# Feed-forward layers as seven products of half blocks, with the residual and the inner operands in DRAM

## The chip, the cores and the metric

The kernel runs on one core of one Trainium2 chip. The metric is the time on the device of one execution, in microseconds (us); lower is better. Engines are named as in the profile: PE (matrix products), DVE (VectorE), ACT (ScalarE), POOL (GpSimd), SP (the queue that issues the DMAs).

## The reference, cut to what matters

A decoder of two layers over 1024 tokens of width 1024, all in float32. Each layer is `x += mixer(RMSNorm(x))`, then `x += SwiGLU(RMSNorm(x))`. The mixer of layer 0 has sixteen attention heads of two kinds, that of layer 1 eight differential heads; the change doesn't touch what they compute. The feed-forward part, which it does touch, has an inner width of 2816:

```python
def swiglu(h, w_gate, w_up, w_down):
    a = jnp.einsum('bsd,df->bsf', h, w_gate)
    u = jnp.einsum('bsd,df->bsf', h, w_up)
    return jnp.einsum('bsf,fd->bsd', jax.nn.silu(a) * u, w_down)
```

## The kernel before, in words

Activations lie transposed: 128 rows of the width by partition, the tokens along the row, in two halves of 512 (`th` 0 and 1). A float32 product is made of three passes in a one-pass number format: an operand x is split into a high part, which ACT writes as a cast, and a low part, which DVE or POOL writes as x minus the high part; `mm3` (L365) then issues high times high, high times low and low times high (L369, L370, L371) for each 128 rows of the contraction, a stationary block of 128 x 128 against a moving one of 128 x 512.

**Mixer.** `mixer` (L797) runs eight windows of attention, with projections and most of the output projection filled in between. `out_rest` (L963) follows it: the last two pieces' part of the output projection (6 matmuls for each of 16 pieces of x), the sum with x on DVE (L984), and `prep` (L306) of each piece: ACT multiplies by the norm's gain into the high part, DVE writes the low part (L315), ACT squares, and DVE or POOL adds up the squares (L321). `rms` (L324) makes 1 / rms of a half's tokens from that sum: a DVE add (L329), a split, two matmuls (L334, L335), Ln and Exp on ACT, and a Newton step on DVE (L343 to L345), into the row tile `rt`.

**Feed-forward.** The feed-forward (`ffn`, L1021) takes x times gain as it is and brings 1 / rms in behind the product, so its matmuls don't wait for `rms`. It goes through the inner width in groups of three or two chunks of 128. Of each chunk, `ffn_half` (L994) issues 24 matmuls for gate and 24 for up, for each half of the tokens; DVE, ACT, POOL (L1005) and DVE make silu(gate) times up, and ACT and DVE split it. Then `down` (L1011) multiplies the group's chunks into all eight pieces of the output and adds each result to x, which stays in SBUF (L1018, one operand in PSUM). Of layer 0's last group, `prep` and `rms` of the next norm follow piece by piece. In matmuls, gate and up are 22 chunks x 2 x 2 halves x 24 = 2112, down is 22 x 8 x 2 x 3 = 1056: 3168 in each layer.

**Weights.** `w_load` (L204) brings each weight tile by DMA into one of three raw tiles and splits it, the low part on DVE while a feed-forward runs and on POOL otherwise (`pool_split`); `w_ahead` keeps two to four tiles ahead, across the border between a feed-forward and the next mixer.

**Order and memory.** The text writes a program order. The framework then lays out each engine's instructions when it builds: among those that it expects to be ready it takes the one that stands first in the text. The order is fixed from then on; each engine and the SP queue go through theirs one by one, and wait where an operand isn't there. SBUF is 44 tiles of 4 KB by partition and some of 2 KB, made once, handed out and taken back by `Slots` (L48).

## Time and profile before

| | us |
|---|---|
| three runs | 2703.07, 2704.07, 2707.98 |
| median | 2704.07 |
| profiled execution, first to last instruction (span) | 2704.3 |
| PE busy in it | 2621.7 |
| DVE, ACT, POOL busy in it | 1550.8, 1111.2, 416.5 |

The page gives no other time of the profiled execution than its span; that is 0.2 us above the median of the runs. Busy time is a sum over the whole span; the feed-forward parts lie at about 660 to 1400 us and 1975 to 2701 us, the mixers ahead of each. A line number in a row is that of the code before; helpers (L84 and L92 are ACT's) gather many places under one line.

### The profile page before, as it was taken

Reading aid. Unit: us, or ns where it says so; the run is one execution under the profiler, and the core shown is the slowest. Engines: PE = TensorE matmul, PEld = TensorE weight load, DVE = VectorE, ACT = ScalarE, POOL = GpSimd, SP = SyncE. Lnnn points to the kernel's source line nnn. Section 1 sums busy time; section 2 is a strip of 40 time slices with the busy share of each in tenths; the row PEclk is TensorE's granted clock in tenths of the full one; section 3 lists DMA queues with packets and bytes.
Section 4 is the critical chain, followed back from the end, with each engine's and each line's share of the span. In section 5 each row is a group of like instructions: output and inputs, shape, how many; then the busy total and the mean of one; then the engine's idle time right before and its main releaser. Section 6 shows DMA issues by size and latency. Waiting matters only on the chain. (4 is left out here: it accounts for less than half of the span.)

```text
span 2704.3 us, 34626 instructions
## 1 busy us (share of the span) xinstructions
PE 2621.7 (97%) x12688; PEld 2159.9 (80%) x12688; DVE 1550.8 (57%) x3095; ACT 1111.2 (41%) x2276; POOL 416.5 (15%) x400
## 2 busy tenths in 40 slices
PE   8898899999999999999999999998999999999999
PEld 7776788777888888888878877876778888888887
DVE  6879868988333334333376687788663334333343
ACT  5656676755311211111156666676451211121111
POOL 4112111211100000000022232323110000000000
PEclk9999999999999999999999999999999999999999
DMA  5323042552111111111133232335311111111112
GB/s 182 85 61 80 28 129 79 146 172 81 50 52 46 49 47 53 49 40 55 43 121 86 77 97 74 80 100 156 125 39 45 50 47 55 48 43 54 46 50 79
DMA packets 118310, 202.61 MB, mean 75 GB/s; under 512 B 14163, under 2 KB 44660, under 8 KB 118140
## 3 DMA queue, kind: packets, MB, share of 16 engines
q1 hardware_dynamic: 118140, 200.41, 24.5%
q8 instruction: 99, 1.62, 0.2%
q14 instruction: 71, 0.58, 0.1%
HBM read 135.83 MB, written 22.58 MB: 59 GB/s over the span
## 5 line engine op out<-in xcount | busy, mean ns | idle before, releaser
L369 PE MATMUL bk<-sr,sr 128*128 128x512 f32 x2880 | 1129.7, 393 | 7.5 <-DVE hf L422 3.2
L370 PE MATMUL bk<-sr,sr 128*128 128x512 f32 x2880 | 1128.0, 392 | 4.2 <-DVE sr L922 4.2
L371 PE MATMUL bk<-sr,sr 128*128 128x512 f32 x2880 | 1126.7, 391 | 0.0
L369 PEld LDWEIGHTS bk<-sr,sr 128*128 128x128 f32 x2880 | 542.4, 188 | 121.7 <-DVE sf L1018 5.0
L370 PEld LDWEIGHTS bk<-sr,sr 128*128 128x128 f32 x2880 | 541.8, 188 | 114.1 <-DVE sr L922 5.8
L371 PEld LDWEIGHTS bk<-sr,sr 128*128 128x128 f32 x2880 | 542.1, 188 | 110.1 <-issue 0.4
L84 ACT CAST sr<-raw 128x512 fp32r<-128x512 f32 (+2 forms) x436 | 253.6, 587 | 648.2 <-PE bk L370 540.6
L218 DVE TENSOR_TENSOR sr<-raw,sr 128x512 fp32r<-128x512 f32 (+1 forms) x304 | 197.4, 650 | 237.0 <-ACT sr L84 221.6
L1005 POOL TENSOR_TENSOR hf<-hf,rt 128x512 f32<-128x512 f32 x88 | 114.4, 1300 | 1267.9 <-ACT hf L92 1267.9
L1018 DVE TENSOR_TENSOR sf<-bk,sf 128x512 f32<-128x512 f32 x256 | 176.2, 689 | 183.0 <-PE bk L371 182.7
L218 POOL TENSOR_TENSOR sr<-raw,sr 128x512 fp32r<-128x512 f32 (+2 forms) x132 | 177.0, 1349 | 354.6 <-ACT sr L84 171.5
L92 ACT ACTIVATE hf<-hf 128x512 f32<-128x512 f32 x200 | 125.5, 629 | 250.7 <-DVE hf L1003 247.9
L84 ACT CAST sr<-hf 128x512 fp32r<-128x512 f32 (+1 forms) x158 | 98.1, 621 | 294.7 <-DVE hf L1006 269.7
L1006 DVE TENSOR_TENSOR hf<-hf,bk 128x512 f32<-128x512 f32 x88 | 60.6, 688 | 252.9 <-PE bk L371 248.5
L560 PE MATMUL bk<-sr,sr 128*128 128x512 f32 (+2 forms) x768 | 200.0, 357 | 4.8 <-ACT sf L92 4.3
L682 PE MATMUL bk<-hr,sr 128*128 128x512 f32 (+2 forms) x560 | 166.0, 389 | 12.9 <-DVE hr L700 12.2
L84 ACT CAST hr<-bk 128x512 fp32r<-128x512 f32 (+2 forms) x240 | 122.4, 527 | 97.6 <-PE bk L668 86.7
L700 DVE TENSOR_TENSOR hr<-bk,hr 128x512 fp32r<-128x512 f32 (+2 forms) x240 | 142.3, 604 | 34.7 <-ACT hr L84 33.4
L1003 DVE TENSOR_TENSOR hf<-bk,rt 128x512 f32<-128x512 f32 x88 | 60.9, 691 | 172.2 <-PE bk L371 172.2
L560 PEld LDWEIGHTS bk<-sr,sr 128*128 128x128 f32 x768 | 127.9, 190 | 29.4 <-ACT sf L92 16.0
L462 PE MATMUL bk<-sr,sr 128*128 128x256 f32 (+1 forms) x512 | 147.2, 289 | 2.8 <-DVE sr L315 2.7
L668 PE MATMUL bk<-ident,sf 128*128 128x128 f32 x768 | 134.3, 276 | 15.3 <-DVE sf L580 11.4
(148 smaller groups left out, 2787.8 us busy)
## 6 DMA issues: line engine op xcount, KB each, us to landing
sr<-sr SPq DMA_DIRECT2D x96, 256.0 KB, 3.0
raw<-in_wg_dram SPq DMA_DIRECT2D x88, 256.0 KB, 2.8
raw<-in_wu_dram SPq DMA_DIRECT2D x88, 256.0 KB, 2.7
raw<-in_wd_dram SPq DMA_DIRECT2D x72, 256.0 KB, 2.7
raw<-in_w_dram SPq DMA_DIRECT2D x64, 256.0 KB, 2.9
sr<-sr SPq DMA_DIRECT2D x128, 128.0 KB, 2.3
sf<-od SPq DMA_DIRECT2D x14, 512.0 KB, 3.5
raw<-in_wd_dram SPq DMA_DIRECT2D x48, 128.0 KB, 2.2
```

The costliest lines, as they stand in the source:

```text
L84: self.last = self.e.copy(out, in_)
L92: self.last = self.e.activation(*args, **kw)
L218: (self.nc.gpsimd if self.pool_split else self.nc.vector).tensor_tensor(r32(l[:, m]), r, h[:, m], ALU.subtract)
L369: nc.tensor.matmul(ps, WH[k], hH[k], start=first and k == 0, stop=False)
L370: nc.tensor.matmul(ps, WH[k], hL[k], start=False, stop=False)
L371: nc.tensor.matmul(ps, WL[k], hH[k], start=False, stop=last and k == n - 1)
L462: nc.tensor.matmul(ps[:, 0:n], hl, vh[k], start=False, stop=k == KC - 1)
L560: nc.tensor.matmul(b[:, 0:hi - lo], r32(Q[i // 4][:, q]), r32(KK[:, lo:hi]), start=j == 0, stop=j == 1)
L668: nc.tensor.transpose(t[:, (i - 4 * g) * P:(i - 4 * g + 1) * P], w[:, kb * P:kb * P + P], self.ident[:])
L682: nc.tensor.matmul(ps[:, c1:], x, y, start=first and j == 0, stop=last and j == len(terms) - 1)
L700: self.nc.vector.tensor_tensor(r32(l[:, c0:]), src, h[:, c0:], ALU.subtract)
L1018: self.nc.vector.tensor_tensor(x, ps[:], x, ALU.add)
```

## The change: what it does

Each feed-forward product is written as a product of 2 x 2 half blocks, C = A B, and made of seven block products instead of eight (Strassen's method in the form with 15 sums). Of gate and up, A is a chunk of the two weights (rows: gate, up; columns: the even and the odd 128-row pieces of x) and B the normed x (rows: even and odd pieces; columns: the two halves of the tokens). Of down, A is a pair of chunks of its weight (rows: the two halves of the output's width; columns: the two chunks) and B the inner result of that pair.

- The work is a list of stages, each prepared (`prep_gate`, `prep_down`) and run (`gate`, `down`): 11 batches of two chunks x 7 products with 24 matmuls each, then three groups of 4, 4 and 3 pairs x 7 products with 12 matmuls for each pair. That is 1848 + 924 = 2772 matmuls in a layer. Preparing of gate and up goes three stages ahead, of down one.
- POOL makes the sums of weights (`left`: three at product 2, one at product 5, for each chunk or pair). ACT and DVE split every operand of every product (`split`).
- Products share PSUM banks in the order 0+1, 2+3, 4+5, 6 (down: 0+1, 2+3, 6, 4+5): the second product is added onto the first once ACT or DVE has taken the first out. `rE` has all eight banks.
- `out_rest` sends x to `y_dram`, no longer makes `prep`, and needs 1 / rms before it multiplies: x times gain times `rt` on DVE, in place, then split into B; the sums of B (two on DVE, two on POOL for each of four pieces) and their splits follow once both halves are there. 28 tiles of B stay for the layer.
- The inner result's seven operands of a pair (`hidden`: four DVE sums) go to `t_dram` and come back as they are needed (`take_right`).
- The output's x comes from `y_dram`, is added and goes back, for each group and piece (`add_x`: DVE where the product is in PSUM, POOL elsewhere); with the last group it goes to the output, or to `x_dram` and into the next `prep`.
- Feed-forward weights no longer pass through `w_load`; they are loaded whole (512 KB) and split by product. The weights of layer 1's mixer are no longer loaded during the feed-forward by the text.
- `Slots` hands out places, for which a new tile is made each time, and the pools are joined during a feed-forward. The raw tiles are four, of which the mixer holds one for what was `row3`.

```diff
+    def left(self, i, A, tmp):
+        p = self.nc.gpsimd
+        a11, a12, a21, a22 = A
+        if i == 2:
+            p.tensor_tensor(tmp, a21, a22, ALU.add)
+            p.tensor_tensor(a21, a11, a21, ALU.subtract)
+            p.tensor_tensor(a11, tmp, a11, ALU.subtract)
+        if i == 5:
+            p.tensor_tensor(a12, a12, a11, ALU.subtract)
+        return self.split((a11, a12, a11, a21, tmp, a12, a22)[i])
...
+    def split(self, x):
+        t = self.sr.get()
+        h, l = t[:, 0:TH], t[:, TH:2 * TH]
...
+        self.S.copy(r32(h), x)
+        self.nc.vector.tensor_tensor(r32(l), x, h, ALU.subtract)
+        return t
...
     def out_rest(self, l):
...
+        Slots.join(self.sr, self.sf)
+        Slots.join(self.hr, self.hf, self.raw)
+        self.take_raw(0)
...
                 nc.vector.tensor_tensor(x, ps[:], x, ALU.add)
-                if k < 6:
-                    self.prep(acc, x, G_FFN0 if l == 0 else G_FFN1, th, k)
-            for k in range(6, KC):
-                self.prep(acc, self.x_at(k, th), G_FFN0 if l == 0 else G_FFN1, th, k)
+                nc.sync.dma_start(self.y_dram[k][:, sl], x)
+                self.squares(acc, x, k, k < 2)
             self.rms(acc, th)
+            for k in range(KC):
+                x = self.x_at(k, th)
+                nc.vector.scalar_tensor_tensor(x, x, self.gains[:, g0 + k:g0 + k + 1], self.rt[:, sl],
+                                               ALU.mult, ALU.mult)
+                if th == 0:
+                    self.B[k % 2].append(self.split(x))
+            if th == 0:
+                self.prep_to(2)
...
+        for b11, b12, b21, b22 in xs:
+            nc.vector.tensor_tensor(b11, b12, b11, ALU.subtract)
+            nc.gpsimd.tensor_tensor(b12, b22, b12, ALU.subtract)
+            self.B[5].append(self.split(b22))
+            nc.vector.tensor_tensor(b22, b22, b11, ALU.subtract)
+            self.B[2].append(self.split(b22))
+            nc.gpsimd.tensor_tensor(b21, b21, b22, ALU.subtract)
+        for i, place in ((3, 1), (4, 0), (6, 2)):
+            for j in range(4):
+                self.B[i].append(self.split(xs[j][place]))
...
+    def gate(self, b, i, W):
...
+            if i == 0:
+                v["p"], v["s"] = self.hf.get(), self.hf.get()
+                self.S.copy(v["p"][:], ps)
+            elif i == 1:
+                self.S.activation(v["s"][:], ps, AF.Silu)
+            elif i == 2:
+                v["u"] = self.hf.get()
+                nc.vector.tensor_tensor(v["u"][:], ps, v["p"][:], ALU.add)
...
+            elif i == 5:
+                u = v["u"][:]
+                nc.vector.tensor_tensor(u, ps, u, ALU.add)
+                self.S.activation(u, u, AF.Silu)
+                nc.gpsimd.tensor_tensor(u, u, v["q"][:], ALU.mult)
+            else:
+                nc.vector.tensor_tensor(v["p"][:], ps, v["p"][:], ALU.add)
+                nc.gpsimd.tensor_tensor(v["s"][:], v["s"][:], v["p"][:], ALU.mult)
...
+    def down(self, g, s, ops):
...
+            if i == 0:
+                self.S.copy(p0, ps)
+            elif i == 1:
+                self.add_x(g, u, 0, ps, True)
+            elif i == 2:
+                nc.vector.tensor_tensor(u2, ps, p0, ALU.add)
+            elif i == 3:
+                nc.vector.tensor_tensor(p0, ps, p0, ALU.add)
+            else:
+                c = self.hf.get()
+                nc.vector.tensor_tensor(c[:], ps, u2 if i == 5 else p0, ALU.add)
+                self.add_x(g, 4 + u if i != 5 else u, 0 if i == 6 else 1, c[:], False)
+                self.hf.put(c)
...
+    def add_x(self, g, k, th, c, psum):
...
+        t = self.hf.get()
+        nc.sync.dma_start(t[:], self.y_dram[k][:, sl])
+        (nc.vector if psum else nc.gpsimd).tensor_tensor(t[:], c, t[:], ALU.add)
+        dst = self.y_dram[k] if not last else self.x_dram[k] if self.l == 0 else self.out[k * P:(k + 1) * P, :]
+        nc.sync.dma_start(dst[:, sl], t[:])
```

## Rows read from the trace of the kernel before

**Rows 1.** The page, part 1: engine, busy us (share), instructions.

```profile
PE 2621.7 (97%) x12688; PEld 2159.9 (80%) x12688; DVE 1550.8 (57%) x3095; ACT 1111.2 (41%) x2276; POOL 416.5 (15%) x400
```

**Rows 2.** Windows of 50 and 10 us: length, engines' busy us, granted clock, DMA share, GB/s.

```profile
670.00:680.00 10.00, 7.25 (x28) 5.59 (x27) 7.82 (x12) 5.61 (x7) 1.94 (x2) 0.89 0.20 66
...
700.00:750.00 50.00, 50.00 (x222) 41.39 (x221) 19.16 (x30) 11.42 (x19) 3.88 (x3) 1.00 0.17 58
...
2650.00:2700.00 50.00, 50.00 (x223) 41.38 (x222) 19.30 (x29) 6.25 (x10) 3.90 (x3) 1.00 0.23 83
```

**Rows 3.** Groups by line, PE alone, 690 to 1340 us.

```profile
L369 PE MATMUL bk<-sr,sr 128*128 128x512 f32 x956 | 371.9, 389 | 0.0
```

**Rows 4.** Groups by line and shape: busy us, mean ns, idle before and its releasers.

```profile
L84 ACT CAST sr<-raw 128x512 fp32r<-128x512 f32 x364 | 224.3, 622 | 603.7 <-PE bk L370 500.6 <-PE bk L371 43.0 <-DMA raw<-in_wu_dram 18.8
L218 DVE TENSOR_TENSOR sr<-raw,sr 128x512 fp32r<-128x512 f32 x256 | 177.0, 692 | 215.1 <-ACT sr L84 199.7 <-PE bk L370 13.0 <-PE bk L371 1.4
L1018 DVE TENSOR_TENSOR sf<-bk,sf 128x512 f32<-128x512 f32 x256 | 176.2, 689 | 183.0 <-PE bk L371 182.7
...
L1005 POOL TENSOR_TENSOR hf<-hf,rt 128x512 f32<-128x512 f32 x88 | 114.4, 1300 | 1267.9 <-ACT hf L92 1267.9
```

**Rows 5.** Timeline at layer 0's border, DVE and POOL: start us, us, engine, line.

```profile
641.25 0.74 DVE L315 SCALAR_TENSOR_TENSOR sr<-sf,gains,sr 128x512 fp32r<-128x512 f32 x1
...
651.38 0.68 DVE L984 TENSOR_TENSOR sf<-bk,sf 128x512 f32<-128x512 f32 x1
651.87 1.29 POOL L321 TENSOR_TENSOR sf<-sf,hf 128x512 f32<-128x512 f32 x1 [3.70 <-issue]
651.98 1.73 DVE L315 SCALAR_TENSOR_TENSOR sr<-sf,gains,sr 128x512 fp32r<-128x512 f32 x1
...
656.16 0.68 DVE L329 TENSOR_TENSOR sf<-sf 128x512 f32<-128x512 f32 x1
656.76 1.28 DVE L984 TENSOR_TENSOR sf<-bk,sf 128x512 f32<-128x512 f32 x2
...
662.51 0.69 DVE L343 SCALAR_TENSOR_TENSOR hf<-bk,hf 128x512 f32<-128x512 f32 x1
...
665.88 0.68 DVE L345 TENSOR_TENSOR rt<-rt,hf 128x512 f32<-128x512 f32 x1
```

**Rows 6.** PE's waits at layer 0's two borders: us, times, longest.

```profile
PE bk L334 <- ACT hr L84: 4.5, 2, 2.8
...
PE bk L369 <- DVE sf L1018: 3.0, 3, 1.6
PE bk L334 <- ACT hr L84: 2.1, 1, 2.1
```

**Rows 7.** Timeline of PE behind a wait of layer 0's border.

```profile
676.26 0.50 PE L334 MATMUL bk<-hr,sub 128*128 128x512 f32 x1 [2.75 <-ACT hr L84]
...
678.17 0.63 PE L371 MATMUL bk<-sr,sr 128*128 128x512 f32 x1
678.60 0.63 PE L369 MATMUL bk<-sr,sr 128*128 128x512 f32 x1
```

**Rows 8.** DMA, 500 to 640 us: queue (packets, MB, share); issues (KB, us to landing).

```profile
q1 hardware_dynamic: 11730, 22.94, 51.5%
...
pd<-hf SPq DMA_DIRECT2D x12, 256.0 KB, 2.7
sf<-pd SPq DMA_DIRECT2D x12, 256.0 KB, 3.5
```

**Rows 9.** Timeline of the SP queue: loads of x (L949), stores of sums (L954).

```profile
546.67 0.33 SPq L949 DMA_DIRECT2D hf<-in_xT_dram  x1
...
549.24 0.38 SPq L949 DMA_DIRECT2D sf<-in_xT_dram  x1
...
551.62 0.33 SPq L954 DMA_DIRECT2D pd<-hf  x1
```

More of the change, by code (lines that the diff above doesn't have):

```diff
@@ L114, in __init__ @@
         self.p_dram = [dr.tile([P, S], F32, name=f"pd{i}") for i in range(KC)]
+        self.y_dram = [dr.tile([P, S], F32, name=f"yd{i}") for i in range(KC)]
+        self.t_dram = [dr.tile([P, 7 * TH], F32, name=f"td{i}") for i in range(NF // 2)]
         self.c_dram = dr.tile([8, S], F32, name="cd")
@@ L176, in make_weights @@
         tail(a["wo0r"])
-        self.ffn_weights(seq, 0)
         vq(a["w1v"], 0)
@@ new lines, in products @@
+    def products(self, ps, WT, BT, c, first, last):
+        nc = self.nc
+        n = len(WT)
+        for j in range(n):
+            w, b = WT[j], BT[j]
+            wh, wl = r32(w[:, c]), r32(w[:, TH + c.start:TH + c.stop])
+            bh, bl = r32(b[:, 0:TH]), r32(b[:, TH:2 * TH])
+            nc.tensor.matmul(ps, wh, bh, start=first and j == 0, stop=False, skip_group_check=True)
+            nc.tensor.matmul(ps, wh, bl, start=False, stop=False, skip_group_check=True)
+            nc.tensor.matmul(ps, wl, bh, start=False, stop=j == n - 1, skip_group_check=True)
@@ new lines, in feed_forward @@
+    def feed_forward(self, l):
+        self.l = l
+        self.B = [[] for _ in range(7)]
+        self.raws, self.downs = {}, {}
+        self.v, self.ps, self.tmp, self.tmps = [{}, {}], [None, None], [None, None], None
+        self.todo, self.made = list(self.stages()), []
+        self.out_rest(l)
+        n = len(self.todo)
+        for i, (_, run, _) in enumerate(self.todo):
+            ahead = i + 1
+            while ahead < n and ahead - self.todo[ahead][2] <= i:
+                ahead += 1
+            self.prep_to(ahead)
+            run(self.made[i])
+            self.made[i] = None
+            if l == 0 and i == n - 3:
+                self.rms(self.acc, 0, True)
+        if l == 0:
+            self.rms(self.acc, 1, True)
+            self.sf.put(self.acc)
+        Slots.part((self.sr, N_R), (self.sf, N_F))
+        Slots.part((self.hr, N_HR), (self.hf, N_HF), (self.raw, N_RAW))
```

310 lines of the change are left out of this document (195 added, 115 removed).

## The prediction

> **What bounds the kernel now.** The page's first part comes first: PE is busy for 2621.7 us, 97% of the span of 2704.3 [rows 1]. The share is an average, so the windows come next. In the feed-forward parts PE is busy for all 50 us of a window while DVE has 19 and POOL 4, at a granted clock of 1.00, in the first such window as in the last [rows 2]. Grouped by line over 690 to 1340 us, each of the three passes has 956 matmuls and no idle time: 650 / 2868 = 0.2266 us for each [rows 3]. So here a matmul less is 0.2266 us less, until another engine becomes the bound. The prediction is about when that happens.
>
> **What the change removes.** 3168 - 2772 = 396 matmuls in a layer, 792 in all, of the same shape: 792 x 0.2266 = **-179.5 us**.
>
> **What it adds, and beside what.** Prices: a split is 0.62 on ACT and 0.69 on DVE; a sum taken out of PSUM is 0.69 on DVE; a two-input operation on POOL is 1.30 [rows 4]. They don't simply run side by side. L315 reads two SBUF operands and takes 0.74 alone, but 1.73 where it begins within a POOL operation of 1.29; L984, with one operand in PSUM, keeps its 0.68 beside the same operation [rows 5]. I read it so: DVE operations on two SBUF operands and POOL operations exclude each other, those out of PSUM don't.
>
> *Gate and up*, a batch: PE 168 x 0.2266 = 38.1 us. POOL has 8 weight sums and 4 products, 12 x 1.30 = 15.6; DVE on two SBUF operands has 14 splits and 4 sums, 18 x 0.69 = 12.4. Together 28.0 of 38.1, and DVE's 10 operations out of PSUM (6.9) and ACT's 12.5 fit beside them. Three stages of preparing ahead (16 us) cover the rest. The wait that is added is that of a second product for its bank: between two products on one bank PE has the other chunk's 12 matmuls, 2.7 us, and the take-out of 0.69 may stand behind one DVE operation held up by POOL (1.30 + 0.69). That just fits. Ends: nothing, or one held-up operation at each of 3 pairs of 22 batches, 66 x 0.69 = 45. I take **+10**, near the lower end, because the sum of both fits.
>
> *Down*, a group of four pairs: PE 336 x 0.2266 = 76.1 us. POOL has 16 weight sums and 12 sums of x, 28 x 1.30 = 36.4; DVE has 56 splits, 38.6; together 75.0 that exclude each other, and DVE's 24 operations out of PSUM, 16.6. If those all fall into POOL's time, nothing is lost; if none does, 91.6 - 76.1 = 15.5. Of the group of three: 31.2 + 29.0 = 60.2 against 57.1, and 76.8 with the 16.6, so 3.1 to 19.7. The half of the 16.6 gives 7.2 + 7.2 + 11.4 = 26 for a layer; POOL's first sums can be made in the gate stages' spare time, so I take 20: **+40** for both layers, ends 0 and 2 x 50.7 = 101.
>
> The DMAs lie beside this. A group of four pairs moves 8 x 512 + 28 x 256 + 32 x 256 KB = 19.9 MB in 76 us, 262 GB/s; its last three stages 11.5 MB in 32.6 us, 354 GB/s. At 500 to 640 us the queue moved 22.94 MB with 51.5% of the DMA engines' time, so 318 GB/s at 100% [rows 8]: the last three stages are over it by 3.6 us, which the stages ahead can hold.
>
> *The border from mixer to feed-forward.* Here the deferred 1 / rms goes, and PE must wait for a normed x. Count from the first matmul of `out_rest`, all terms in us. Its 96 matmuls end at 21.8. The first half's squares are summed at 13; `rms` took from L329 at 656.16 to L345's end at 666.56, 10.4 [rows 5], so `rt` is there at 23. Then DVE scales and splits eight pieces, 8 x (0.74 + 0.69) = 11.4: to 35. The second half's `rms` stands behind that in the text and becomes ready only at 24, so it gets DVE at 34 and ends at 44. Eight scalings more: 50. Product 2 needs, for each of four pieces, two sums and two splits on DVE, 4 x 2.75 = 11, with eight POOL sums beside it that exclude them, up to 10.4: its last operand comes at 61 to 71, say 65, and its last matmuls end at 66. Without waits its 72 matmuls after `out_rest` end at 21.8 + 16.3 = 38. Lost: 28; products 0 and 1 lie inside the wait. Before, the waits for the two L334 cost 4.5 [rows 6]. Behind such a wait the matmuls start 0.43 apart instead of 0.23 [rows 7], at a granted clock of 0.89 over that window [rows 2], so partly at the lower level, 1.2 GHz: some eight matmuls, 1.6 us, twice. 28 - 4.5 + 3 = 26.5 in each layer: **+53**. Ends: POOL out of the way and `rms` unhindered gives 18, POOL's eight sums and the six weight sums of the first batch all in front gives 38; so 36 to 76.
>
> *Layer 0's end.* The last three stages have PE 108 x 0.2266 = 24.5 us. Beside it stand 12 POOL sums (15.6), 12 L315 (8.9), ten additions of squares (5 x 1.30 + 5 x 0.68 = 9.9) and three weight sums (3.9): 38.3, so 13.8 late, and the next mixer's weights are split on POOL behind that, no longer ahead. The first half's projections cover some of it, as before, where 3.0 + 2.1 were waited for [rows 6]. **+8**, ends 0 and 25. *Layer 1's end*: a POOL sum and a split take-out behind the last product, 1.30 + 0.69: **+2**.
>
> *Mixers*: the same work. Places that come free whole, not by parts, and the missing load-ahead can shift waits either way; their PE idle time is the 82.6 of the span less 14 at the borders, and a tenth of it is 7. I take 0.
>
> *The SP queue* gets 68 issues a group at 0.33 [rows 9], 22 of 76 us. A store of a sum waits for POOL, and what stands behind it waits too. In the code before, the same pattern (load x, add, store) was laid out with loads ahead: two L949 stand before the store L954 [rows 9]; and the second half's L984 runs before the first half's L343 [rows 5]. So I cost it at nothing; the rival below has its price.
>
> Sum: -179.5 + 10 + 40 + 53 + 8 + 2 = -66.5. Against the profiled 2704.3, which is the median of the runs but for 0.2: **2638**.
>
> **Rivals.**
> A. *Down hides all*: preparing runs ahead into the stages without POOL work (products 1 and 3 of a group), as by my count of the code 24 places are free there. Then only the borders and ends are lost: 2704.3 - 179.5 + 53 + 4 = 2582. For it: the sums that exclude each other just fit. Against: the last three stages of a group don't.
> B. *The bank pairs bind*: PE waits at nearly every pair of gate and up, 45 instead of 10, and down waits 60 instead of 40: 2693. For it: a margin of 2.7 - 2.0; against: two of three times the DVE is free.
> C. *DVE and POOL become the bound, slower than before*: none of DVE's operations out of PSUM falls into POOL's time, for in a fixed order the next one is often a split that POOL holds up. Place: the 21 down stages of a layer. Price: 101, with layer 0's end at 25: -179.5 + 10 + 101 + 53 + 25 + 2 = +11.5, so 2716. It decides once a down part loses over 47 us in a layer. The store that holds up the SP queue would act at the same place: a load (3.5) and POOL's 1.30 for each of 12 sums, 57.6 against 32.6 us of PE, 25 a group [rows 8], 150 in all, if the order were that of the text.
> D. *No change by clock*: each of the 42 down stages begins with a wait and pays the 1.6 us of [rows 7]: +67, so 2705. The Trainium skill (TensorE: Matmul & The Clock Gate, HAM oscillation) describes such kernels, whose bursts of matmuls are broken by waits and start again at the lower clock. The trace has it after the long wait of [rows 7] only.
> E. *It doesn't do what it says*: the sevenths' matmuls could take longer each; shapes and passes are those of [rows 3], so I give it nothing.
>
> **How the numbers follow.** Forecast 50%, with its own range 2605 to 2672; A 22%, B 10%, C 13%, D 5%. Less than 0.2% (5.4 us) can't be told from no change. Faster: 50 + 22 + 10 = 82%; within: D, 5%; slower: C, 13%. The range from 2570 to 2715 leaves out half of C and the lower third of A; the ends of all unknown costs together would be 2556 and 2781.
>
> **What would show it.** In the changed profile: 5544 feed-forward matmuls, 0.227 us apart in gate and up with PE busy for 50 of 50 us; PE idle for some 28 us behind each `out_rest`, released by ACT or DVE splits of B; PE idle of some us at a group's first and third down stage, released by DVE splits behind POOL; DVE splits of over 1 us beside POOL. Waits on DMAs of `t_dram` or `y_dram` in front of PE's operands would speak for the SP queue. The prediction is wrong if down loses over 47 us a layer, or if the borders lose under 15 or over 45.

## The result, and the profile after

The changed kernel took 2728.35 us (median of 4 runs, 2726.30 to 2731.51) beside 2706.03 for the kernel before on the same chip: a ratio of 1.0079, interval 1.0065 to 1.0094. It is slower by 0.8%, where 2638 was forecast. The matmuls went as forecast (11896 against 12688, PE's first line of the page, against [rows 1]), but PE is busy for 91% of the span instead of 97%, and POOL, at 15% before, for 35%:

```profile
PE 2482.8 (91%) x11896; PEld 2032.0 (75%) x11896; DVE 1906.0 (70%) x3411; ACT 1287.8 (47%) x2598; POOL 958.8 (35%) x760
```

The windows of layer 0 answer to [rows 2] (length; busy us of PE, PEld, DVE, ACT, POOL; granted clock; DMA share; GB/s). The first lies in the border from mixer to feed-forward, the second in gate and up, the third in down:

```profile
700.00:750.00 50.00, 19.43 (x74) 15.15 (x75) 44.70 (x56) 18.59 (x33) 19.77 (x13) 0.64 0.12 42
770.00:1140.00 370.00, 370.00 (x1634) 306.39 (x1633) 220.62 (x281) 119.74 (x203) 157.99 (x111) 1.00 0.34 120
1141.00:1393.00 252.00, 222.72 (x933) 180.06 (x931) 179.99 (x238) 104.33 (x182) 119.90 (x81) 0.95 0.56 187
```

Gate and up, the largest part, loses nothing: PE is busy throughout, at full clock. Most of the loss is in the two short parts around it. Added up over gaps between matmuls, PE's idle time rose from 75.7 to 233.7 us, by 158.0: 41 at each of the two borders (115 us from the first sum of `out_rest`: 4.7 to 45.9 and 46.1), 27 and 25 behind them, all in down (nothing there before), 5.3 and 9.5 in the two mixers, 8.5 at the first layer's end. And PE's busy time fell by 138.9, not by 179.5, so the matmuls that are left took 40.6 longer: in the border the granted clock is 0.64, between the levels of 1.2 and 2.4 GHz. 158.0 - 138.9 = 19.1, of 20.8 in the spans.

The waits show what PE stands for. At the border (PE's waits, 648 to 770 us: total, times, longest) it is splits, in two long waits:

```profile
PE bk L1138 <- ACT sr L102: 22.9, 3, 15.5
PE bk L1139 <- DVE sr L1031: 22.8, 4, 18.9
```

The timeline there shows DVE making the sums of the half blocks (L1012, L1015) and the splits (L1031), and POOL its own (L1013, L1017):

```profile
719.57 0.68 DVE L1031 TENSOR_TENSOR sr<-sf,sr 128x512 fp32r<-128x512 f32 x1
720.17 1.75 DVE L1012 TENSOR_TENSOR sf<-sf,sf 128x512 f32<-128x512 f32 x1
722.44 1.75 DVE L1015 TENSOR_TENSOR sf<-sf,sf 128x512 f32<-128x512 f32 x1
...
719.73 1.64 POOL L1017 TENSOR_TENSOR sf<-sf,sf 128x512 f32<-128x512 f32 x1 [0.63 <-DVE sf L1015]
722.00 1.64 POOL L1013 TENSOR_TENSOR sf<-sf 128x512 f32<-128x512 f32 x1 [0.63 <-DVE sf L1012]
```

Each waits for the other: a sum on two SBUF operands takes 1.75 on DVE beside one of 1.64 on POOL. In down (1141 to 1393 us) PE's own waits are these, beside the closing norm's (L339):

```profile
PE bk L1051 <- ACT sf L102: 12.6, 4, 5.2
PE bk L339 <- ACT hr L102: 7.4, 1, 7.4
PE bk L1051 <- DVE sf L1231: 6.7, 1, 6.7
```

So PE doesn't wait for an operand there. It waits for a bank: product 1 is added onto product 0 once ACT has copied that out, product 3 onto product 2 once DVE has (L1231). The copies come late because of what stands ahead of them in ACT's row, as in the first group:

```profile
1152.26 2.89 ACT L102 CAST sr<-sf 128x512 fp32r<-128x512 f32 x5 [8.21 <-POOL sf L1062]
1155.05 1.55 ACT L102 COPY sf<-bk 128x512 f32<-128x512 f32 x3
```

The first of the casts is of product 2's weights, and ACT stood 8.21 us ahead of it for POOL's sum; PE, which waits for the first copy, started again at 1155.68. The waits of ACT, DVE and the SP queue over the same window show that as a chain:

```profile
ACT sr L102 <- POOL sf L1062: 44.3, 9, 8.2
ACT sr L102 <- DMA sf<-in_wd_dram: 16.3, 3, 11.1
...
DVE sr L1031 <- ACT sr L102: 51.8, 25, 8.6
...
SPq L1254 <- POOL hf L1252: 72.1, 29, 7.6
```

ACT's half of a split waits for POOL's weight sums, and DVE's half for ACT's. The SP queue stands longest of all, behind POOL's sum of y (L1252); how much of PE's loss hangs on each, the runs must say.

### The profile page after: what moved, and what is told of

Read it like the earlier page. It is cut to its first block, busy times and chain, and to the rows that moved or that the text cites. A ratio compares the mean times of both kernels' runs of the same rounds, so it can differ in the third digit from the quotient of the medians.

```text
span 2725.1 us, 35163 instructions
## 1 busy us (share of the span) xinstructions
PE 2482.8 (91%) x11896; PEld 2032.0 (75%) x11896; DVE 1906.0 (70%) x3411; ACT 1287.8 (47%) x2598; POOL 958.8 (35%) x760
## 4 chain that ended last, share of the span: by engine, by line
PE 65%; DVE 15%; ACT 5%; POOL 5%; DMA 5%; issue 4%; SPq 1%; POOLq 0%; DVEq 0%; ACTq 0%
PE bk L1139 10%; PE bk L1138 10%; PE bk L1140 10%; PE bk L375 4%; PE bk L376 4%; PE bk L374 4%; PE bk L1051 3%; PE bk L1052 3%; PE bk L1053 3%; PE bk L687 3%; PE bk L565 3%; DVE sf L583 2%; PE bk L673 2%; ACT sf L110 1%; DVE sr L1031 1%
## 5 line engine op out<-in xcount | busy, mean ns | idle before, releaser
L102 ACT CAST sr<-sf 128x512 fp32r<-128x512 f32 (+1 forms) x690 | 409.4, 620 | 777.8 <-PE bk L1140 309.0
L1031 DVE TENSOR_TENSOR sr<-sf,sr 128x512 fp32r<-128x512 f32 x628 | 515.3, 847 | 166.4 <-ACT sr L102 165.1
L1138 PE MATMUL bk<-sr,sr 128*128 128x512 f32 x1232 | 483.7, 394 | 46.7 <-ACT sr L102 45.7
L1139 PE MATMUL bk<-sr,sr 128*128 128x512 f32 x1232 | 483.9, 393 | 45.8 <-DVE sr L1031 45.8
L1140 PE MATMUL bk<-sr,sr 128*128 128x512 f32 x1232 | 481.8, 391 | 0.0
L374 PE MATMUL bk<-sr,sr 128*128 128x512 f32 x768 | 307.0, 400 | 4.9 <-ACT sr L102 2.7
L1138 PEld LDWEIGHTS bk<-sr,sr 128*128 128x128 f32 x1232 | 233.1, 190 | 100.3 <-ACT sr L102 50.0
L375 PE MATMUL bk<-sr,sr 128*128 128x512 f32 x768 | 305.6, 398 | 2.3 <-DVE sr L928 2.3
L1139 PEld LDWEIGHTS bk<-sr,sr 128*128 128x128 f32 x1232 | 233.2, 189 | 98.3 <-DVE sr L1031 50.4
L376 PE MATMUL bk<-sr,sr 128*128 128x512 f32 x768 | 304.0, 396 | 1.2 <-POOL sr L220 1.2
L220 POOL TENSOR_TENSOR sr<-raw,sr 128x512 fp32r<-128x512 f32 (+2 forms) x140 | 189.1, 1365 | 314.8 <-ACT sr L102 181.5
L1051 PE MATMUL bk<-sr,sr 128*128 128x512 f32 x616 | 249.2, 405 | 46.3 <-ACT sf L102 30.8
L1140 PEld LDWEIGHTS bk<-sr,sr 128*128 128x128 f32 x1232 | 233.0, 189 | 48.6 <-DVE sr L1031 0.4
L1052 PE MATMUL bk<-sr,sr 128*128 128x512 f32 x616 | 246.9, 401 | 0.0
L1053 PE MATMUL bk<-sr,sr 128*128 128x512 f32 x616 | 246.2, 400 | 0.0
L1252 POOL TENSOR_TENSOR hf<-hf,hf 128x512 f32<-128x512 f32 x72 | 106.3, 1485 | 257.5 <-DVE hf L1236 245.7
L1051 PEld LDWEIGHTS bk<-sr,sr 128*128 128x128 f32 x616 | 120.1, 195 | 77.6 <-ACT sf L102 35.0
L374 PEld LDWEIGHTS bk<-sr,sr 128*128 128x128 f32 x768 | 145.3, 189 | 33.9 <-ACT sr L102 3.7
```

Source lines behind the costliest of these rows:

```text
L102: self.last = self.e.copy(out, in_)
L374: nc.tensor.matmul(ps, WH[k], hH[k], start=first and k == 0, stop=False)
L375: nc.tensor.matmul(ps, WH[k], hL[k], start=False, stop=False)
L376: nc.tensor.matmul(ps, WL[k], hH[k], start=False, stop=last and k == n - 1)
L1031: self.nc.vector.tensor_tensor(r32(l), x, h, ALU.subtract)
L1051: nc.tensor.matmul(ps, wh, bh, start=first and j == 0, stop=False, skip_group_check=True)
```

## The experiments

PE's loss in down is told by stage: the time from one stage's first matmul to the next one's, less 0.2267 for each matmul. After the change it is 41.7 us in layer 0 and 36.0 in layer 1; 13.4 of the 41.7 are in the stages of products 4 and 5 of the last group, beside the closing norm, the rest in the first stages of each group. "Gate 168" is the start of the 168th gate matmul, counted from the first sum of `out_rest` in layer 0: 111.8 after the change, of which 53 are lost. Times are medians; ratios are against the kernel before.

| run | us | ratio, interval | gate 168 | down, layers 0, 1 |
|---|---|---|---|---|
| after | 2728.4 | 1.0079 (1.0065 to 1.0094) | 111.8 | 41.7, 36.0 |
| m1 places | 2721.6 | 1.0050 (1.0034 to 1.0067) | | |
| m3 mixers' tiles | 2711.9 | 1.0022 (1.0012 to 1.0032) | 112.1 | 38.3, 36.6 |
| e1 PE's order | 2731.1 | 1.0082 (1.0063 to 1.0101) | 113.1 | 41.7, 35.6 |
| e2 + late Silu | 2727.2 | 1.0074 (1.0059 to 1.0089) | 112.2 | 41.1, 35.9 |
| e3 + product 2 first | 2732.2 | 1.0097 (1.0082 to 1.0112) | 115.3 | 41.5, 35.6 |
| e4 = e2, no weight sums | 2720.1 | 1.0053 (1.0038 to 1.0068) | 108.6 | 42.3, 33.2 |
| d3 stores from POOL | 2744.7 | 1.0136 (1.0121 to 1.0151) | 112.0 | 49.6, 40.5 |
| d1 y added ahead | 2730.5 | 1.0088 (1.0073 to 1.0103) | 112.1 | 51.7, 34.7 |
| d2 no y | 2711.9 | one run | 111.8 | 35.8, 27.7 |
| c1 = m3, down's order | 2701.1 | 0.9981 (0.9972 to 0.9991) | 112.2 | 48.5, 20.6 |
| c2 + border | 2689.1 | 0.9940 (0.9923 to 0.9958) | 103.3 | 45.8, 21.2 |
| c3 + layer end | 2683.0 | 0.9913 (0.9899 to 0.9928) | 104.4 | 41.2, 18.5 |
| c4 + border's weights | 2675.2 | 0.9880 (0.9863 to 0.9896) | 102.4 | 41.2, 18.6 |
| f3 + DVE's order | 2669.9 | 0.9864 (0.9848 to 0.9881) | 99.2 | 41.8, 19.6 |
| f2 = f3, no sums | 2645.1 | one run | 99.1 | 31.0, 7.1 |
| g1 = f3, sums on DVE | 2626.3 | 0.9705 (0.9692 to 0.9718) | 94.0 | 23.5, 9.9 |
| g2 = after, sums on DVE | 2656.4 | 0.9817 (0.9801 to 0.9834) | 108.3 | 13.3, 0.7 |
| h1 = g1, no pins in down | 2612.4 | 0.9654 (0.9641 to 0.9668) | 94.5 | 12.0, 0.7 |

**The mixers.** m1 takes the change's `Slots` into the kernel before; m3 takes it out of the mixers of the kernel after.

```diff
 # m1, on the kernel before
-        t = self.free.popleft()
+        i = self.free.popleft()
+        t = self.pool.tile([P, self.width], F32, tag=f"p{self.width}_{i}", ...)
 # m3, on the kernel after; join() sets fix to None, part() to {}
+        t = self.fix.get(i) if self.fix is not None else None
+        if t is None: t = self.pool.tile(...)
```

> The kernel before with one part of the change alone: every place of the pool hands out a new tile each time it is taken (the framework then waits for the whole old tile), where before one tile per place lived through the kernel; feed-forward layers, order of the text and everything else as before. Theory P (the places cost the mixers): the first sum of the output projection's rest, at 639.3 us in the profile before and 648.5 after the change, comes at about 648, the second mixer is about 12 us longer as well, and the time is 2720 to 2730. Rival R (the mixers lose to something else, such as the memory traffic and the laid-out order that the new feed-forward layers bring): 639 to 641 at that place and 2703 to 2709 in all.

> After the change, but in the two mixers each place keeps one tile, as before the change; from the output projection's rest to the end of the feed-forward layer each taking of a place is a new tile, as changed. The run of the places alone put 9.7 us on the first mixer and 9.9 on the second. If that is all that the mixers lost: first sum of the rest at 639 to 641 us (648.5 after the change), second mixer 510 to 513 us from its first scores to that sum (523.2), and 2705 to 2711 in all. Rival (the second mixer loses to the places that the feed-forward layer leaves in another order): the first mixer alone comes back, 2716 to 2720.

The first sum of `out_rest` in m1, then m3, one timeline row each:

```profile
648.96 0.68 DVE L1001 TENSOR_TENSOR sf<-bk,sf 128x512 f32<-128x512 f32 x1
```

```profile
641.46 1.49 DVE L1001 TENSOR_TENSOR sf<-bk,sf 128x512 f32<-128x512 f32 x2
```

It came at 639.3 before and 648.5 after. So the places alone cost the first mixer what the change did, and m1's second mixer (first scores to first sum) took 520.7 us against 510.8. Theory P holds for the mixers: some 20 us, none of it Strassen's. In m1's whole time 14.6 of them show (2721.6 against 2707.0 on the same chip), and with the tiles kept 16 come back, a little less than expected (2711.9, not 2705 to 2711).

**The border, by order.** e1 and e2 pin instructions behind others; e3 lays the border's sums differently.

```diff
 # e1: every product of the first pair behind the one before it, on TensorE
+            with self.tc.issue_after(self.pe_last.ins):
+                self.products_gate_(ps, w, B, i)
 # e2: and its Silu behind the second half's norm, on ScalarE
+                    with self.tc.issue_after(self.rms_last.ins):
                         self.S.activation(v["s"][:], ps, AF.Silu)
 # e3: and product 2's operands first, into tiles of their own
+            nc.vector.tensor_tensor(b11, b12, b11, ALU.subtract)
+            nc.vector.tensor_tensor(t[:], b22, b11, ALU.subtract)
+            self.B[2].append(self.split(t[:]))
```

> After the change, with the first pair's fourteen products pinned on TensorE in the order of the text, so that none stands before an earlier one; nothing else touched. Theory O (the wait of 18.9 us in front of the fourth product is the price of TensorE's order): products 2 and 3 run in that wait, up to 19 us per layer come back, 2690 to 2700. Theory S (the whole border waits for the slowest operand, at 730.5 us in the profile, whatever the order; only what fits into the gap before it is saved): 10.9 us of products move into the gap at half clock or less, 3 to 6 us per layer come back, 2716 to 2723.

> As the run with TensorE's order pinned, and the first pair's Silu of product 1 is also laid out behind the second half's norm on ScalarE, so that no Silu comes between its Ln and Exp. Theory T (the two extra table loads of 1.28 us and the Silus, about 6 us in the 13.1 us of that norm, are on the chain of the border): the norm takes 8 to 9 us, the last operand of product 2 is 4 to 5 us earlier, and the time is 8 to 10 us below that of the run with the order alone. Rival (the scalings and splits behind it, bound by DVE beside POOL, take the gain): within 3 us of that run.

> The run with order and late Silu, with the border's sums put in another order: DVE makes the four operands of product 2 (two sums and a split each) ahead of all else, POOL's sums and the splits for products 3 to 6 follow. Theory C (what TensorE waits for is the row of DVE operations up to product 2's last operand, 24.5 us from the last scaling in that run, of which 8 sums and 4 splits, some 11 us, are needed): TensorE resumes at 66 to 70 us after the first sum instead of 82, the 168th gate matmul comes at 98 to 102 instead of 112, and 20 to 28 us come back over two layers, 2698 to 2707. Rival K (the clock, low after the idle time, and the operands of products 3 to 6 take the gain): 108 to 112 and 2718 to 2727.

PE's longest border wait in e1, and in e3:

```profile
PE bk L1145 <- ACT sr L102: 39.3, 4, 31.2
```

```profile
PE bk L1158 <- ACT sr L102: 40.7, 4, 31.3
```

e1 turns the two waits of 15.5 and 18.9 into one of 31.2 and gives nothing: theory S was nearer, and even its 3 to 6 us are not there. It also took the Silus out from between Ln and Exp, so that e2's own edit had little left to do: the second norm's scalings end at 61.9 after the change, at 58.2 in e1 and at 57.5 in e2, and PE resumes at 83.3, 82.6 and 82.0. Of 4.4 us gained ahead of it 1.3 reach PE: the row of DVE operations behind the scalings takes the rest. In e3 that row was shorter, its last split for product 2 ending at 76.1, but PE resumed at 85.0: it waited for the weight of product 2, whose tile took the place of an x tile that came free with the border's last splits. So e3 doesn't decide on theory C.

e4 leaves POOL's weight sums of the first pair out:

```diff
+        if bare:                       # first pair of a layer
+            return self.split((a11, a12, a11, a21, a11, a12, a22)[i])
```

> The run with order and late Silu, with POOL's eight weight sums of the first pair of each layer left out (their products then use a plain block, so that part of the result is not computed). Theory X (a DVE operation beside a POOL one takes 1.5 to 1.75 us instead of 0.7 to 0.9, and these sums lie inside the norm and the scalings): scaling and splits of the first half end 3 to 5 us earlier, the second norm too, TensorE resumes 5 to 8 us earlier, 2712 to 2718. Rival (the border sums of POOL are the ones that matter): within 3 us per layer, 2722 to 2727.

PE resumed 4.2 us earlier than in e2 (77.8 instead of 82.0), gate 168 came 3.6 earlier and the time fell by 7.1: theory X, a little short of its 5 to 8 and of its time (2720.1, not 2712 to 2718). c2 and c4 then have the weights of products 2 and 3 made ahead of the second norm, with the operands of product 2 pinned in a row on DVE:

```diff
 # c2, on c1, with e1, e2 and e3
-                self.prep_to(2)
+                self.prep_to(3)                 # c4: prep_to(4)
+            keep = self.tc.keep_in_program_order   # the two sums and the split of e3
 # c4: places for it
-        if i == 1 and b + 1 < self.BATCHES:
+        if i == (4 if b == 0 else 1) and b + 1 < self.BATCHES:
```

> The run with the down stages' order, and the border as well: first pair's products in the text's order on TensorE, Silu behind the second norm, the four operands of product 2 made first with the eight sums, the splits and their order pinned on DVE, and product 2's weights made before the second half's norm instead of behind the border's sums (in the run with product 2's operands first, TensorE waited to 85 us for that weight's split, whose place came free late). Theory C (the row of DVE operations up to product 2's last operand is what binds): TensorE resumes at 66 to 72 us after the first sum, the 168th gate matmul comes at 98 to 104 (112 after the change), 16 to 28 us less than the run with the down order alone. Rival K (clock, POOL's sums, operands of the later products): 108 or more and within 8 us of that run.

> The run before it in this call, with product 3's weights also made before the second half's norm, and the second pair's raw weights fetched three stages later so that places are free for it. In the run with the border TensorE resumed at 66 us after the first sum and stood again for 9.9 us at 72.8 for a split on ScalarE. Theory P (that split is of product 3's weights, whose place came free only when the border's last sums were split): the wait goes, the 168th gate matmul comes at 94 to 98 instead of 103.4, 10 to 18 us less in all. Rival (it is product 3's right operand, the sums of POOL, each 1.7 to 2.5 us): within 4 us, and if the second pair's weights come too late, slower.

PE's border waits in c2, and in c4:

```profile
PE bk L1173 <- ACT sr L109: 27.1, 8, 9.9
```

```profile
PE bk L1174 <- ACT sr L109: 18.3, 7, 7.1
PE bk L1174 <- DVE hf L1143: 6.6, 1, 6.6
```

c2 brings gate 168 to 103.3, theory C. Its time fell by 12.0, less than the 16 to 28 expected: the two mixers took 8 longer than in c1. c4 takes ACT's wait of 9.9 away, as theory P said, and 6.6 of it comes back as a wait for the sum that takes product 2 out of PSUM (L1143), which stood behind the splits for products 3 to 6 on DVE: 2 us of gate 168 gained, where 5 to 9 were expected, and 7.8 of time, where 10 to 18 were.

**Down, by queue and by order.** d3 and d1 take the stores of y from behind POOL, d2 leaves y out of the first two groups:

```diff
 # d3
-        nc.sync.dma_start(dst[:, sl], t[:])
+        (nc.sync if psum else nc.gpsimd).dma_start(dst[:, sl], t[:])
 # d1: y loaded at the stage's start, POOL adds the base; behind the product
+        nc.vector.tensor_tensor(t[:], ps, t[:], ALU.add)
 # d2
+        if last:                       # load and store of y in the last group only
```

> After the change, with the stores of the 16 POOL-made sums of each down group issued from POOL's own queue right behind the add, instead of from SP, where the store waits and holds up the loads behind it (72.5 us in 30 waits of the profile, longest 7.6). Theory Q (SP's queue makes down late): TensorE's loss in down, 41.8 and 36 us, falls by 20 or more per layer, 2680 to 2690. Theory X (DVE's splits beside POOL and the transfers' own durations make it late): 2722 to 2732; slower still if POOL's issuing takes its time from the weight sums.

> After the change, with the old sum y loaded at the start of a down stage, POOL adding the base (p0 or u2) to it while TensorE still multiplies, and one DVE sum from PSUM behind the product; before, DVE made product plus base and POOL added y behind it. Counts per engine are the same. Theory Q (POOL's sum behind the product holds SP's stores, and these the loads of the next stages): SP's waits for POOL fall from 72.5 us to under 20, TensorE's loss in down from 42 and 36 us to 15 to 25 each, 2690 to 2705. Theory X (sharing of DVE and POOL, or the transfers): down stays within 5 us per layer, 2718 to 2735.

> After the change as it was, without the load and store of the old sum y in the first two down groups (32 loads and 32 stores per layer; the sum is made with another operand, so that part of the result is not computed). Theory Q of the forecast (SP's queue stands behind those stores, 25 us a group at worst): the loss in down, 41.7 and 36.0 us, falls by 15 or more per layer. Theory H (the laid-out order on ScalarE and POOL): it falls by under 8 per layer, most of it in the first group's third stage (6.9), whose weights were issued behind such a store.

The SP queue's waits in down, of d3 and of d1:

```profile
SPq L1251 <- DMA yd<-hf: 60.7, 17, 10.7
```

```profile
SPq L1257 <- DVE hf L1255: 46.5, 28, 5.5
```

Of the 72 us behind POOL's sum of y 18.1 are left in d3 and 6.7 in d1, and the queue stands behind something else; PE gains nothing. Without y 5.9 and 8.3 us are gained: the first group's third stage alone gives 6.9 and 6.6, and other stages lose or gain a little. There ACT waited 11.1 us for weights of the *next* group, whose split the framework had laid ahead. DVE's take-out of product 2 stood behind that, which is PE's wait of 6.7. SP issued these weights some 7 us late, behind a load of y that waited for the landing of a store of y (its wait is the longest, 5.8, in the first line, SP's waits over 1141 to 1393 us):

```profile
SPq L1251 <- DMA yd<-hf: 19.7, 11, 5.8
...
1170.79 0.32 SPq L1254 DMA_DIRECT2D yd<-hf  x1
1177.16 0.32 SPq L1251 DMA_DIRECT2D hf<-yd  x1
...
1178.05 0.38 SPq L1170 DMA_DIRECT2D sf<-in_wd_dram  x1
...
1183.42 1.14 ACT L102 CAST sr<-sf 128x512 fp32r<-128x512 f32 x2 [11.07 <-DMA sf<-in_wd_dram]
```

So the queue is some 6 to 8 us of a layer's 42 and 36, from one run. c1 goes for the order, c3 for the layer's end, f3 for DVE's order:

```diff
 # c1: splits and POOL's sums of a down stage, and the norm one stage later
+        if self.pin:
+            self.tc.keep_in_program_order(self.S.last); self.tc.keep_in_program_order(y)
-            if l == 0 and i == n - 3:
+            if l == 0 and i == n - 2:
 # c3, on c2
+                self.acc.append(self.sf.get())            # (1) a sum for each half
+ self.rE = Rot([b[7], b[4], b[5], b[6], *b[0:4]])         # (1) banks
+        if s == 1: ...  p(tmp, a21, a22, ALU.add)         # (2) two sums a stage earlier
+                self.w_ahead(2, 4)                        # (3) at i == n - 2
 # f3, on c4
+        self.pin = self.l == 1 or g < 2
+            if i == 2: self.late()     # splits of B[5], B[6] behind product 2's sum
```

> The run with the mixers' tiles kept (2711.9 us), with two edits in the down stages: the splits and POOL's weight sums of a stage are pinned behind what the text has before them on their engine, so that no split for a later group stands in front of one for the next stage; and the first layer's closing norm of its first half is put one stage later (behind product 4, not behind product 6). Theory H (ScalarE stands in order behind a split for the next group whose weights are not there yet, 11.1 us at 1183.4 in the profile after, and POOL behind sums for a later stage, so that SP's store behind it holds the loads 8 us): of the loss in down by stage, 13.9 us in the first group's first four stages, 10.4 in the second's first two and 4 to 13.6 in the third's first two, half goes, 12 to 18 us per layer; and of the 13 us in the stages of product 4 and 5 of the first layer's last group, due to the norm, 8 to 12 go. Together 30 to 45 us, 2667 to 2682. Rival B (the transfers themselves are late, at 0.75 of the DMA engines' time in the busiest stretch): only the norm's 8 to 12, 2699 to 2705. Rival Z (pinned behind sums that wait for TensorE, the splits come later): slower than 2712.

> The run with the border (2689.1 us) with three more edits. (1) The closing norm of the first layer has a sum of its own for each half, is put behind product 4's stage, and the down stages' banks rotate from 7, 4, 5, 6, 0 to 3, so that products 4 and 5 no longer accumulate in the two banks that the norm uses. (2) POOL's first two weight sums of a down group (8 of 12) are made one stage earlier. (3) The next mixer's first four weight tiles are loaded and split during the first layer's last two stages, as before the change. Theory N (the norm's banks): the loss of the last group's last stages in the first layer, 21 to 28 us with the order pinned, 13.4 as changed, falls below 6. Theory S (POOL's 12 sums in a row, some 17 us, are late for product 2): the 8.6 us of the first group's second stage and the 1.2 and 2.4 of the second's go to under 4 together, 8 us per layer. Theory W (weights): from the last feed-forward product to the first scores 62 us become 45 to 50. All three: 2636 to 2655. If none holds, 2685 to 2692.

> The fastest run so far (2675.2 us) with three edits of the laid-out order. In the border the splits for products 5 and 6 are pinned on DVE behind the sum that takes product 2 out of PSUM, and those for product 4 behind product 3's; in that run all stood ahead of it, and TensorE stood 6.6 us at 71.7 us after the first sum for it. In the first layer's last down group nothing is pinned, so that the sums that take product 4 out of PSUM need not stand behind the splits of product 5 (12.9 us of TensorE). Theory O (DVE's order): gate 168 at 96 to 99 instead of 102, the last group's stages of product 4 and 5 lose under 8 us instead of 16.5, together 14 to 22 us, 2653 to 2661. Theory X (DVE's operations beside POOL's, 1.7 us instead of 0.6 to 0.7, fill the same time in any order): within 5 us of 2675.

In c1 and c2 the closing norm of layer 0 reads its first half's sum of squares after part of it has been written over by the other half's, so that part of the result is another; the operations are the same in number. c1's layer 1 loses 20.6 instead of 36.6, as theory H said. In layer 0 the loss rose to 48.5: with the norm a stage later, product 5's stage alone loses 21.2. So the time, 2701.1, is not theory H's (2667 to 2682); it lies where rival B had it (2699 to 2705), by another way. c3's theory N fails: 13.0 and 3.5 stay in these stages, as after the change (10.0 and 3.4), whatever the banks. Theory S fails as well (7.8 instead of 8.6 in the first group's second stage, where PE now waits for product 1's own splits). The weights loaded ahead gave 7 us between down's last product and the first scores, half of what was expected. f3 gives 3 us at the border and nothing in down, 5 us of time, at the edge of the rival: in layer 0 the last group's two stages beside the norm fell from 16.5 to 12.0, but the second group's sixth rose from 1.6 to 10.1.

**POOL's sums themselves.** f2 leaves the weight sums of the first group out of f3:

```diff
+        if s is not None and self.bare:      # bare: the first group
+            return self.split((a11, a12, a11, a21, a11, a12, a22)[i])
```

> The run before it in this call, with POOL's 16 weight sums of the first down group of each layer left out (its products then use plain blocks, so that part of the result is not computed). If POOL's sums are late for product 2, or slow the splits of DVE beside them, the 7.8 us of the first group's second stage go to 0 to 2, 12 to 16 us in all. By the durations of the splits in that stage the two are told apart: 1.7 us beside POOL and 0.6 to 0.7 without it. If it is the td loads behind a store in SP's queue, 7 to 8 us stay.

The first group's loss, 9 us in layer 0 and 10.5 in layer 1, went to nothing, and the time fell by 25 us, more than the 12 to 16 expected. DVE's splits around the first group's second stage (duration in ns min/median/max, first and last start), in f3 and in f2:

```profile
L1061 DVE TENSOR_TENSOR sr<-sf,sr x11: 1552/1770/1780, 1128.0 to 1144.9; 128x512 fp32r<-128x512 f32 x11
```

```profile
L1061 DVE TENSOR_TENSOR sr<-sf,sr x18: 682/684/693, 1125.5 to 1144.5; 128x512 fp32r<-128x512 f32 x18
```

g1 has the sums again, but made by DVE, and the border's sums as well; g2 does that, and nothing else, to the kernel after; h1 takes the pins in down out of g1 and puts the two early sums back where they were.

```diff
 # g2, on the kernel after
-            nc.gpsimd.tensor_tensor(b12, b22, b12, ALU.subtract)
+            nc.vector.tensor_tensor(b12, b22, b12, ALU.subtract)
-            nc.gpsimd.tensor_tensor(b21, b21, b22, ALU.subtract)
+            nc.vector.tensor_tensor(b21, b21, b22, ALU.subtract)
-        p = self.nc.gpsimd
+        p = e or self.nc.gpsimd              # e: nc.vector from prep_down
 # h1, on g1
-        self.pin = self.l == 1 or g < 2 or s < 5
```

> The fastest run so far (2669.9 us) with the weight sums of the down stages (16 a group, 12 in the last) and the border's eight sums of POOL made on DVE, where such a sum of two SBUF operands takes 0.68 us when POOL rests; nothing else in down is on POOL but the adding of the old sum y. In the first layer's last group only the last two stages stay unpinned. Theory X (DVE beside POOL is what is left in down: splits of 1.770 us beside a sum and 0.684 without): a POOL sum of 1.3 to 1.6 us costs DVE about 1.1 us, made on DVE it costs 0.68, and the chain from a sum to its split loses a hand-over; the loss in down of the second layer goes from 19.6 to 6 to 12 us, the border's 168th gate matmul comes 2 to 6 us earlier than 98.8, and the time is 2635 to 2655. Rival (DVE becomes the bound of down: 11 us more a group on an engine that already does 56 splits and 28 sums from PSUM): 2670 or more.

> After the change as it was (2728.4 us), with one edit: the weight sums of the down stages and the border's eight sums of POOL made on DVE. In the run that had all the order's edits ahead of it this took 44 us, 23 of them in down and 10 in the border. Theory X first (DVE beside POOL is the larger cause): 2685 to 2700, the loss in down 41.7 and 36.0 us falls to under 22 each. Theory H first (the order on ScalarE holds the same stages whatever DVE does, and the gain shows only behind the pins): 2710 to 2725, the loss in down stays over 28 each; and as DVE then stands in order for those sums too, slower is possible.

> The fastest run (2626.3 us) without the pins of the down stages and with the two early sums back in product 2's stage; the border's pins, the mixers' tiles, the weights loaded ahead, the norm's banks and the sums on DVE stay. If the pins were only a way around POOL's late sums: the loss in down falls from 23.5 and 9.9 us to at most 13 and 2, and the time to 2605 to 2618. If the order on ScalarE is a cause of its own: down loses as much or more, 2624 to 2640.

g1 came out as theory X had it, and somewhat better (2626.3; gate 168 at 94.0; 9.9 us in layer 1's down). The one edit of g2 takes 72 us off the kernel after, to 29 us below the lower end of its expectation, and leaves nothing of the loss in down but the 13.3 beside the closing norm. Its down of layer 0, first the window, then the waits of ACT, DVE and the SP queue:

```profile
1138.00:1363.00 225.00, 214.23 (x934) 175.44 (x932) 195.09 (x277) 104.85 (x182) 61.86 (x41) 0.98 0.62 212
```

```profile
ACT sr L102 <- DVE sf L1062: 20.2, 8, 4.2
...
DVE sr L1031 <- ACT sr L102: 15.4, 17, 2.7
...
SPq L1254 <- POOL hf L1252: 58.9, 31, 5.9
```

None of PE's waits for a copy out of product 0 or product 2 is left. The SP queue still stands 58.9 us behind POOL's sum of y, and the DMA share is 0.62 instead of 0.56: neither the queue nor the transfers made PE wait by themselves.

The splits of that stretch by line (count, busy us, mean ns, idle before), after the change, then in g2:

```profile
L1031 DVE TENSOR_TENSOR sr<-sf,sr 128x512 fp32r<-128x512 f32 x137 | 115.2, 879 | 52.1 <-ACT sr L102 51.8
```

```profile
L1031 DVE TENSOR_TENSOR sr<-sf,sr 128x512 fp32r<-128x512 f32 x137 | 107.2, 817 | 15.7 <-ACT sr L102 15.4
```

DVE is busy for longer (195 us of 225 instead of 180 of 252) and PE waits less. The splits' shorter durations are 8 us of busy time; the larger part is that DVE no longer stands waiting, 15.4 instead of 51.8 us, because ACT waits 20.2 for the sums instead of 44.3. Which part of that is the duration of POOL's sums, which their place in POOL's row and which the splits beside them, these runs don't part. h1 then falls to 2612.4: the pins, worth 16 us of layer 1's down in c1, cost 11 and 9 us here, together with the early sums. Theory H was no cause of its own: the order of ACT's row costs something while the sums are late.

h1 is the version to keep, 3.5% below the kernel before and 4.2% below the change as it was (0.9654 / 1.0079). Its page, and its border's wait:

```profile
PE 2474.1 (95%) x11896; PEld 2026.9 (78%) x11896; DVE 1944.5 (74%) x3515; ACT 1281.7 (49%) x2594; POOL 812.8 (31%) x656
```

```profile
PE bk L1186 <- ACT sr L109: 14.2, 6, 6.5
```

## Why the prediction was wrong

*The matmuls* (-179.5) held in number, and gate and up were better than forecast: 1680 matmuls in 380.8 us, 0.2267 each, nothing for the +10.

*Down* (+40) was 77.7, and here the step failed. "If those all fall into POOL's time, nothing is lost; if none does, 15.5" weighs sums of times: 75.0 us of DVE and POOL that exclude each other against 76.1 of PE. The exclusion is there, 1.77 against 0.68 us, but with DVE busier still (195 of 225 us in g2) PE loses only what stands beside the norm. What bound was when a result was ready, and what stood behind it. Product 2's weights need POOL's 12 sums one after another; ACT's casts of them wait in its row, and behind them stands the copy that frees the bank for product 1. That wait of a second product for its bank is the one that the forecast priced for gate and up (+10), where it cost nothing; its sum for down leaves the wait out, and there it stopped PE. The loss stands in the first stages of a group, and the later ones, which the forecast found the tightest, lose nothing apart from the norm's. Rival C had the mechanism, a fixed order in which the next operation "is often a split that POOL holds up"; its mark was "over 47 us a layer", and 42 and 36 fell just short of that. The rival's other form, the SP queue (150), is some 6 to 8 a layer (d2): the longest wait of the profile was not the dear one.

*The border* (+53, at most 76) failed as well. It was 2 x (53.5 - 6) = 95, with 6 for the 4.5 of waits and 1.6 of slow matmuls there before. Counted as the forecast counts, from the first matmul of `out_rest`: `rt` at 25.7 (23), the first half scaled and split at 41.8 (35), the second norm at 55.7 (44), its scalings 7.5 on, product 2's last operand at 83.3 (65). Each step of the row is late, 2.7 us at the first and 18.3 at the last. Two things were mis-sized: POOL's weight sums lie inside the norm (e4: 3.6 us), which the forecast had only at the far end of its range, and the framework lays other splits and Silus into the row that was counted as if it ran alone (c2, which puts the row in order, takes 8.9 off gate 168). Ordered and with DVE's own sums it is 17 us shorter (h1), still 8 over the forecast's 28.

*The clock* was priced at 3 us. Over the whole kernel the matmuls took 40.6 longer, at a granted clock of 0.64 in the border and 0.95 in down; this is part of the terms above, not beside them. The term was read off a wait of 2.75 us [rows 6, 7]; the waits that came were 15 and 19. The reading that the trace before has the lower level after that wait only was wrong too: the granted clock is also 0.91 at 1400 to 1420 us and 0.89 at 1985 to 2000.

*The mixers* (0, or 7) lost 21.7. "Places that come free whole, not by parts" was named and not priced; m1 shows 20 of them.

*Layer 0's end* (+8): idle time rose by 8.5, as forecast, apart from the norm's 13.4 in down. Together: -179.5 + 0 + 77.7 + 95 + 21.7 + 8.5 = 23.4, against 20.8 measured. So the 90 us between forecast and time are down (+38), the border (+42) and the mixers (+22), less the 10 of gate and up. The first two are one kind of error: work was priced by an engine's busy time, while each result waits for the whole row ahead of it. Rival C (2716, 13%) had the right direction and, for down, the right place; its time came out near by other terms, since it had the border at 53 and the mixers at nothing.

## What to carry to other kernels

Work moved to an idle engine is not free when another engine's row waits for its result: count when that result is ready and what stands behind it in the waiting row, copies out of PSUM above all, not each engine's total. Before ordering instructions around a late result, make it early: moving the sums of down and border from POOL to a busier DVE (72 us) was worth more than the five edits from c1 to f3 together (42). And when an allocator changes with an algorithm, time it alone on the old kernel.

## What the runs showed of the hardware

A DVE operation with two SBUF operands takes 0.68 to 0.69 us alone and up to 1.77 when it starts while a POOL operation on SBUF runs, while one out of PSUM keeps 0.69 (L994 beside a POOL sum of 1.30). Where DVE's starts first it keeps its 0.68 and POOL's takes 1.64 instead of 1.30 (the rows at 719.57 and 719.73 above). The Trainium skill (SBUF — State Buffer, Who interferes with whom) says that a DVE instruction with two SBUF inputs contends with a GpSimd one that reads SBUF, its second input coming through a shared read interface. The trace agrees, and adds the price: a split beside a POOL sum loses 1.1 us of DVE, more than the 0.68 that DVE takes for the sum itself. An operation with one SBUF operand was held up too: the TENSOR_SCALAR of the norm (L349) took 1.50 beside a POOL sum and 0.42 alone.

A store issued from POOL's queue took 0.56 us of POOL's time in d3, and the loads behind such stores on the same place then waited for their landing, 60.7 us in all (19.7 after the change); the kernel lost 16 us by the edit.
